# A first norm summed from channel blocks, a last norm's sum moved, and x loaded on another queue: two transformer blocks on one core

## The chip, the cores and the metric

The kernel runs on one NeuronCore of a Trainium2 chip. The metric is the device time of one execution in microseconds (us). The engines are named as the profile names them: PE (TensorE, matmul; PEld its weight loads), ACT (ScalarE), DVE (VectorE), POOL (GpSimd), SP (SyncE, which mostly issues DMAs).

## The reference

Two blocks run one after the other on one sequence of 256 tokens of 1024 channels, in float32. The first block has two layers; each is a gated feed-forward, a hybrid mixer, a second feed-forward and a small gated embedding. The second block has a mixer and a feed-forward with a norm before and a norm after it. What matters here is where norms stand:

```python
def rmsnorm(x, g):
    y = xf * lax.rsqrt(jnp.mean(xf * xf, axis=-1, keepdims=True) + EPS)
    return y.astype(x.dtype) * g

# first thing of the program
h = h + 0.5 * swiglu(rmsnorm(h, ffn1_norm[i]), ffn1_wg[i], ffn1_wu[i], ffn1_wd[i])

# last thing of the program
h = rmsnorm_2(x, norm_mlp_pre[l])
f = jnp.square(jax.nn.relu(h @ w_up[l])) @ w_down[l]
x = x + rmsnorm_2(f, norm_mlp_post[l])
```

`swiglu(x, wg, wu, wd)` is `(silu(x @ wg) * (x @ wu)) @ wd`; the feed-forward width is 2816 in the first block and 4096 in the second.

## The kernel before, in words

**Layout.** The stream h lies in SBUF as eight channel blocks (128 channels on the partitions, 256 tokens along the free axis). All weights are cut into 4948 tiles of 128x128 and laid out in DRAM in the order of use, so that one stream of DMAs reads them. The stream comes in pieces: one of 2 tiles, one of 4, then pieces of 8 tiles (512 KB). They are called w0, w1, w2, ... below (`PIECES`, `feed`). The first six land in buffers named `extra`, the later ones in four buffers named `raw`.

**Precision.** A product in float32 is made of three fast matmuls. ACT rounds a piece to its high part (`whi`), DVE subtracts to get the low part (`wlo`); the activations are split in the same way into `hs` (`split_scaled`: the high part on ACT, the low part on DVE). Then each tile takes three matmuls: high by high, high weight by low activation, low weight by high activation (`mm3`, line 237). Five pairs of `whi` and `wlo` exist, so that the piece five later can be split only when PE is through with the older one.

**Order.** The order of instructions on each engine is not written out by hand: generators run against a small clock model (`Flow`) which emits an instruction when the model says that its operand is there. Each engine then runs its list strictly in order. A DMA is issued by the engine whose `dma_start` is called.

**The first norm.** A norm's factor is one number per token, so the matmuls run on h times the gain, and the factor is applied behind them. Elsewhere in the kernel, `square` adds the squares of the eight blocks into a tile `acc` (squares on ACT, sums on DVE), and `colsum` sums over the partitions with matmuls against a tile of ones; their result lies in the bank `side`. For the first norm the kernel before does neither: it loads x a second time, with tokens on the partitions (`xt`, 1 MB, issued behind piece w6), and `first_sums` squares and sums it on ACT in two instructions. In both ways `rsqrt` (DVE, small instructions) and `bcast` (matmuls against `ident` into `side`, then ACT into `row`) follow.

**x and the first matmuls.** x comes in four DMAs, x0 (block 0), x1 (block 1), x2 (blocks 2 and 3) and x3 (blocks 4 to 7), each issued by SP behind the piece of the same number. The first four units (two gates, two ups, `heads_of`) are computed together: for each of the eight blocks, twelve matmuls. w0 and w1 thus hold 18 matmuls, every later piece 24.

**The last norms.** `norm2` in `second` is the norm ahead of w_up_2. Its factor enters only behind w_down_2 (`sq`, waited for by `down` through `r2ev`). It is spawned ahead of w_up_2, with its column sum among the matmuls of w_up_2.

Of the kernel before, what the change touches and what calls it, by code (L numbers as in the profile page):

```python
# [9 lines left out]
F32 = mybir.dt.float32  # L10
# [7 lines left out]
P = 128  # L18
T = 256
# [59 lines left out]
class Event:  # L79
    def __init__(self, on=False):  # L80
        self.on, self.waiting = on, []
# [110 lines left out]


class Build:
    def __init__(self, ctx, tc, xT, xtok, pT, vec, row, wall, out):
        self.tc, self.nc = tc, tc.nc
        self.xT, self.xtok, self.pT, self.vecd, self.rowd, self.wall, self.out = xT, xtok, pT, vec, row, wall, out
        self.flow = flow = Flow()
        self.spawn, self.fire, self.idle = flow.spawn, flow.fire, flow.idle
        pool = lambda name, bufs, **k: ctx.enter_context(tc.tile_pool(name=name, bufs=bufs, **k))  # L200
        self.fix = pool("fix", 1)
        self.big = pool("big", 1)
        self.dram = pool("dram", 2, space=DRAM)
        ps = pool("ps", 1, space=PSUM)
        fix = lambda name, shape, dt=F32: self.fix.tile(shape, dt, name=name)
        ring = lambda name, n, shape, dt=F32: Ring(flow, [fix(f"{name}{i}", shape, dt) for i in range(n)])
        self.banks = Ring(flow, [ps.tile([P, 512], F32, name=f"bank{i}") for i in range(7)])
        self.side = Ring(flow, [ps.tile([P, 512], F32, name="side")])
        self.raws = ring("raw", NR, [P, S * P])
        self.parts = Ring(flow, [(fix(f"whi{i}", [P, S * P], F32R), fix(f"wlo{i}", [P, S * P], F32R)) for i in range(NB)])  # L210

        self.small = [fix(f"small{i}", [P, 8]) for i in range(6)]
        hs0 = fix("hs0", [P, ND, 2 * T], F32R)
        self.hs = Ring(flow, [hs0, fix("hs1", [P, ND, 2 * T], F32R)])
        self.t = ring("t", 4, [P, T])
        self.vv = ring("vv", 3, [P, T])
        self.cv = ring("cv", 6, [P, 16 + T])
        self.sq = ring("sq", 2, [P, T])
        self.acc = ring("acc", 3, [P, T])
        self.rows = ring("row", 4, [P, T])  # L220
        self.small += [None if i == 17 or 18 <= i < 24 else fix(f"small{i}", [P, 8]) for i in range(6, 24)]
        self.vec = fix("vec", [P, NV])
        self.h = fix("h", [P, ND, T])
        self.ident = fix("ident", [P, P])
        self.ones = fix("ones", [P, P])
        self.mask = fix("mask", [P, P])
        self.tb = fix("tb", [P, 4, 32])
        self.gsum = fix("gsum", [P, 8])
        self.shim = fix("shim", [P, 32])
        self.order = []  # L230
        self.table = None
        self.tables = Ring(flow, [None])
        self.roots = Ring(flow, [None])
# [52 lines left out]
    def feed(self):  # L286

        self.ready = [Event() for _ in PIECES]
        self.done = [Event() for _ in PIECES]
        self.at = [None] * len(PIECES)  # L290
        for q, cnt in enumerate(PIECES):
            raw = yield from self.raws.get()
            n, w = int(FIRST[q]), cnt * P
            self.nc.sync.dma_start(raw[:, :w], self.wall[n * P * P:(n * P + w) * P].rearrange("(p w) -> p w", p=P))
            if q < 4:
                a, b = ((0, 1), (1, 2), (2, 4), (4, 8))[q]
                self.nc.sync.dma_start(self.h[:, a:b, :], self.xT[:, a:b, :])
                self.spawn(self.x_here(a, b), self.flow.use("dma", 0.365 * (b - a)) + 2.2)
            if q == 6:
                self.xt = self.big.tile([P, 2, D], F32, name="xt", tag="ya")  # L300
                self.nc.sync.dma_start(self.xt, self.xtok)
                self.spawn(self.first_sums(), self.flow.use("dma", 2.9) + 2.35)
            if q == 9:
                self.nc.sync.dma_start(self.vec[:, self.early:], self.vecd[:, self.early:])
            wait = self.flow.use("dma", w * P * 4 / 360e3) + 2.35
            self.spawn(self.piece(q, raw, w), wait)
# [172 lines left out]
    def norm(self, s, rows, ev):  # L479

        c, y = self.small[8][:, :2], self.small[9][:, :2]
        yield s["ev"]
        self.chains += 1
        if "cols" in s:
            c = s["cols"]
        else:
            yield from self.colsum(s, EPS, D, c)
        yield from self.rsqrt(y, c)
        yield from self.bcast(rows, y)
        self.fire(ev)  # L490
        self.chains -= 1
# [8 lines left out]
    def setup(self):  # L500
        nc = self.nc
        self.early = a = 32
        nc.sync.dma_start(self.vec[:, :a], self.vecd[:, :a])
        self.xev = [Event() for _ in range(ND)]
        self.flow.use("dma", 1.8)
        make_identity(nc, self.ident)
        nc.vector.memset(self.ones, 1.0)
        nc.vector.memset(self.shim, 0.0)

        nc.vector.memset(self.mask, 0.0)  # L510
        nc.gpsimd.affine_select(out=self.mask, in_=self.mask, pattern=[[1, P]], compare_op=ALU.is_ge,
                                fill=NEG, base=0, channel_multiplier=-1)
        self.chains = 0
        self.started = [Event() for _ in PIECES]
        extra = self.big.tile([P, 6, S * P], F32, name="extra", tag="X")
        self.extra = [extra[:, i, :] for i in range(6)]
        more = self.big.tile([P, 8, 8], F32, name="more", tag="more")
        self.small[18:] = [more[:, i, :] for i in range(6)]
        self.raws.free[:0] = self.extra
        for cv in self.cv.free:  # L520
            nc.vector.memset(cv[:, :16], 0.0)
        self.act(self.small[0], self.ones[:, :8], AF.Silu)

    def first(self, op, gain):
        for n in range(ND):
            yield self.xev[n]
            yield from self.split_scaled(op, n, self.h[:, n, :], gain(n))

    def x_here(self, a, b):
        for n in range(a, b):  # L530
            self.fire(self.xev[n])
        yield 0.0

    def first_sums(self):

        out, xt = self.x_ms["cols"], self.xt
        for tt in range(2):
            yield self.act(xt[:, tt, :], xt[:, tt, :], AF.Square, accum_out=out[:, tt:tt + 1])
        yield self.ts(out, out, 1.0 / D, EPS)
        self.fire(self.x_ms["ev"])  # L540

    def ffn(self, layer, which, sp, s, next_gain):

# [434 lines left out]
    def second(self, sp, ss):  # L978
# [283 lines left out]
            yield self.mul(sq, y, y)  # L1262
            self.fire(r2ev)

        self.spawn(norm2())

        def relu(j, b):
            t = yield from self.t.get()
            yield self.act(t, b[:, :T], AF.Relu)
# [10 lines left out]
        for j in range(NF2):  # L1280
            b = bs[j] if j < H else (yield from self.unit("w_up_2", 0, j, nsp, ND))
            self.spawn(relu(j, b))
        self.drop(nsp)

        C = D // 2
# [56 lines left out]
    def main(self):  # L1342
        gain = lambda name, i: (lambda n: self.v(name, i, n))
        sp = yield from self.new_op()
        s = self.x_ms = dict(cols=self.small[23][:, :2], ev=Event())
        self.spawn(self.first(sp, gain("ffn1_norm", 0)))
        for i in range(DEPTH):
            sp, s = yield from self.ffn(i, 1, sp, s, gain("mix_norm", i))
            sp, s = yield from self.mixer(i, sp, s, gain("ffn2_norm", i))
            pop = Operand(self.big.tile([P, 2, 2 * T], F32R, name="p_sp", tag="xd1"))  # L1350
            self.spawn(self.load_p(i, pop))
            sp, s = yield from self.ffn(i, 2, sp, s, gain("ple_norm", i))
            last = i + 1 == DEPTH
            sp, s = yield from self.ple(i, sp, s, pop, None if last else gain("ffn1_norm", i + 1))
            if not last:
                s, = s
        yield from self.second(sp, s)
# [18 lines left out]

def build(nc):
    dram = lambda name, shape, kind="ExternalInput": nc.dram_tensor(name, shape, F32, kind=kind).ap()
    args = (dram("in_x", (P, ND, T)), dram("in_xt", (P, 2, D)), dram("in_p", (DEPTH, P, 2, T)), dram("in_vec", (P, NV)),
            dram("in_row", (1, D)), dram("in_w", (NTILES * P * P,)), dram("out_0", (P, 2, D), "ExternalOutput"))  # L1380
    with tile.TileContext(nc) as tc, ExitStack() as ctx:
        b = Build(ctx, tc, *args)
        b.run()
    return b.order


def pack(inputs, order):
# [27 lines left out]
    for n, (name, layer, k, blk) in enumerate(order):  # L1415
# [11 lines left out]
        views[q][:, n - FIRST[q]] = t  # L1427
    return {
        "in_x": chan(f["x"][0]),
        "in_xt": np.ascontiguousarray(f["x"][0].reshape(2, P, D).transpose(1, 0, 2)),  # L1430
        "in_p": np.stack([chan(f["p"][i, 0]) for i in range(DEPTH)]),
        "in_vec": vec,
        "in_row": np.ascontiguousarray(f["norm_mlp_post_2"]),
# [13 lines left out]
```

## Time and profile before

| | us |
|---|---|
| median of 3 runs | 1822.45 (1811.29 to 1824.0) |
| the profiled execution | 1822.13 |
| its span, first to last instruction | 1820.3 |
| PE busy | 1789.6 |
| DVE busy | 1318.0 |
| ACT busy | 1050.9 |

The span is nearly full of matmuls, so the time changes only where PE stands still, where its clock is low, or where matmuls are added or taken away. The DMA moves 343.83 MB at a mean of 189 GB/s.

### The profile page before, as it was taken

To read this page: it belongs to the slowest core of one execution; us is meant where nothing else is said; L and a number is where in the kernel's file an instruction comes from. 1 tells how busy PE (TensorE), PEld (TensorE's weight loads), DVE (VectorE), ACT (ScalarE), POOL (GpSimd) and SP (SyncE) were. 2 spreads that over 40 slices of the span, in tenths; PEclk is the share of its full clock that TensorE was granted. 3 is DMA by queue.
4 is the path that set the end of the run, shared out by engine and by line. 5 is a ranking of instruction groups with operands and counts; after the bars stand their busy time and mean duration, and the time that the engine had idled before them with its cause. 6 is when DMAs were issued, how large, how long until landed. Compare 5 with 4: busy or idle time off the path is not lost.

```text
span 1820.3 us, 36518 instructions
## 1 busy us (share of the span) xinstructions
PE 1789.6 (98%) x14900; PEld 1749.2 (96%) x14900; DVE 1318.0 (72%) x2236; ACT 1050.9 (58%) x1707; POOL 10.5 (1%) x22
## 2 busy tenths in 40 slices
PE   8999999999999999999999999999999999989997
PEld 7999999999999999999999999999999999889986
DVE  6666789887676666866678988767666689877643
ACT  5444579664555544654457966455554478656542
POOL 0000000000000000000000000000000000000000
PEclk9999999999999999999999999999999999989999
DMA  7666576655666666566657656466666653546552
GB/s 254 192 186 188 169 244 197 199 196 160 201 194 191 192 196 195 176 198 196 195 172 248 196 198 196 161 194 198 203 194 195 195 176 123 183 140 207 187 195 76
DMA packets 92696, 343.83 MB, mean 189 GB/s; under 512 B 10448, under 2 KB 10960, under 8 KB 91376
## 3 DMA queue, kind: packets, MB, share of 16 engines
q1 hardware_dynamic: 90720, 327.25, 57.4%
q0 software_dynamic: 1520, 13.73, 2.1%
q8 instruction: 116, 1.90, 0.4%
q10 hardware_dynamic: 288, 0.52, 0.1%
q14 instruction: 52, 0.43, 0.1%
HBM read 340.31 MB, written 1.15 MB: 188 GB/s over the span
## 4 chain that ended last, share of the span: by engine, by line
PE 91%; DVE 4%; ACT 2%; DMA 2%; issue 1%; SPq 0%; DVEq 0%; ACTq 0%
PE bank L237 90%; DMA raw<-in_w 1%; DVE wlo L244 1%; PE side L237 1%; ACT L266 1%; ACT whi L266 0%; PE bank L734 0%; DMA h<-in_x 0%; DVE cv L257 0%; DVE small L257 0%; DVE hs L257 0%; DVE acc L244 0%; DVE t L244 0%; DVE vv L257 0%; DVE hs L244 0%
## 5 line engine op out<-in xcount | busy, mean ns | idle before, releaser
L237 PE MATMUL bank<-hs,whi 128*128 128x256 f32 x6928 | 1215.0, 280 | 12.4 <-ACT whi L266 7.9
L237 PEld LDWEIGHTS bank<-hs,whi 128*128 128x128 f32 x6928 | 1055.0, 189 | 19.6 <-ACT whi L266 8.2
L244 DVE TENSOR_TENSOR wlo<-raw,whi 128x1024 fp32r<-128x1024 f32 (+1 forms) x602 | 733.0, 1220 | 378.9 <-ACT whi L266 377.5
L266 ACT ACTIVATE whi<-raw 128x1024 fp32r<-128x1024 f32 (+1 forms) x602 | 635.3, 1058 | 637.4 <-issue 320.1
L237 PE MATMUL bank<-hs,wlo 128*128 128x256 f32 x3464 | 965.7, 279 | 1.9 <-DVE wlo L244 1.8
L237 PEld LDWEIGHTS bank<-hs,wlo 128*128 128x128 f32 x3464 | 655.5, 189 | 2.8 <-DVE wlo L244 2.7
L237 PE MATMUL bank<-V,whi 128*128 128x256 f32 x1920 | 329.0, 277 | 0.0
L237 PEld LDWEIGHTS bank<-V,whi 128*128 128x128 f32 x1920 | 290.4, 188 | 0.0
L237 PE MATMUL bank<-V,wlo 128*128 128x256 f32 x960 | 265.8, 277 | 0.0
L237 PEld LDWEIGHTS bank<-V,wlo 128*128 128x128 f32 x960 | 180.2, 188 | 0.0
L237 PE MATMUL bank<-whi,V 128*128 128x512 f32 x256 | 79.8, 392 | 0.0
L244 DVE TENSOR_TENSOR t<-bank,row 128x256 f32<-128x256 f32 x159 | 64.4, 417 | 17.2 <-PE bank L237 11.1
L257 DVE SCALAR_TENSOR_TENSOR cv<-bank,vec,cv 128x253 f32<-128x253 f32 (+2 forms) x144 | 63.6, 474 | 3.8 <-ACT cv L266 3.2
L244 DVE TENSOR_TENSOR vv<-bank,t 128x256 f32<-128x256 f32 x152 | 62.6, 418 | 3.2 <-ACT t L266 2.9
L244 DVE TENSOR_TENSOR V<-vv,V 128x256 fp32r<-128x256 f32 x152 | 62.5, 420 | 1.5 <-ACT V L266 1.2
L266 ACT ACTIVATE V<-vv 128x256 fp32r<-128x256 f32 x152 | 60.1, 403 | 2.6 <-DVE vv L257 1.6
L237 PEld LDWEIGHTS bank<-whi,V 128*128 128x128 f32 x256 | 48.1, 188 | 10.7
L237 PE MATMUL bank<-wlo,V 128*128 128x512 f32 x128 | 50.1, 392 | 0.0
L266 ACT ACTIVATE dec<-dec,tb 128x256 f32<-128x256 f32 (+1 forms) x128 | 49.5, 445 | 0.1
L244 DVE TENSOR_TENSOR acc<-acc,sq 128x256 f32<-128x256 f32 x101 | 42.4, 420 | 8.6 <-ACT sq L266 8.0
L266 ACT ACT_TABLE_LOAD x37 | 47.5, 1283 | 1.3 <-PEq L1442 0.7
L266 ACT ACTIVATE hs<-h,vec 128x256 fp32r<-128x256 f32 x80 | 38.4, 498 | 11.9 <-DMA h<-in_x 7.1
(152 smaller groups left out, 1113.4 us busy)
## 6 DMA issues: line engine op xcount, KB each, us to landing
raw<-in_w SPq DMA_DIRECT2D x613, 512.0 KB, 4.3
dec<-cum_d POOLq DMA_DIRECT2D x8, 1536.0 KB, 10.0
extra<-in_w SPq DMA_DIRECT2D x4, 512.0 KB, 8.6
xt<-in_xt SPq DMA_DIRECT2D x1, 1024.0 KB, 11.5
h<-in_x SPq DMA_DIRECT2D x1, 512.0 KB, 8.6
praw<-in_p POOLq DMA_DIRECT2D x2, 256.0 KB, 4.5
gain<-in_row POOLq DMA_DIRECT2D x1, 512.0 KB, 4.7
out<-o SPq DMA_DIRECT2D x2, 256.0 KB, 2.7
```

The source lines that it names most:

```text
L237: self.nc.tensor.matmul(ps, w, x, start=start, stop=stop, **k)
L244: self.nc.vector.tensor_tensor(out, a, b, op=op)
L257: self.nc.vector.scalar_tensor_tensor(out, a, s, b, op0=op0, op1=op1)
L266: self.nc.scalar.activation(out=out, in_=a, func=func, **k)
```

## The change

x and the first 32 columns of the vector table are loaded by DMAs that ScalarE issues, all at the start of the program. The second copy of x and `first_sums` go away; the first norm takes its squares block by block (`square`), with a column sum on PE (`colsum`) like every other norm. `norm2` is spawned behind w_up_2's loop instead of ahead of it.

```diff
             if q < 4:
-                a, b = ((0, 1), (1, 2), (2, 4), (4, 8))[q]
-                self.nc.sync.dma_start(self.h[:, a:b, :], self.xT[:, a:b, :])
+                a, b = self.xpieces[q]
                 self.spawn(self.x_here(a, b), self.flow.use("dma", 0.365 * (b - a)) + 2.2)
-            if q == 6:
-                self.xt = self.big.tile([P, 2, D], F32, name="xt", tag="ya")
-                self.nc.sync.dma_start(self.xt, self.xtok)
-                self.spawn(self.first_sums(), self.flow.use("dma", 2.9) + 2.35)
...
         yield s["ev"]
         self.chains += 1
-        if "cols" in s:
-            c = s["cols"]
-        else:
-            yield from self.colsum(s, EPS, D, c)
+        yield from self.colsum(s, EPS, D, c)
...
         self.early = a = 32
-        nc.sync.dma_start(self.vec[:, :a], self.vecd[:, :a])
+        self.xpieces = ((0, 1), (1, 2), (2, 4), (4, 8))
+        nc.scalar.dma_start(self.vec[:, :a], self.vecd[:, :a])
+        for b, c in self.xpieces:
+            nc.scalar.dma_start(self.h[:, b:c, :], self.xT[:, b:c, :])
...
-    def first(self, op, gain):
+    def first(self, op, s, gain):
         for n in range(ND):
             yield self.xev[n]
             yield from self.split_scaled(op, n, self.h[:, n, :], gain(n))
+            self.spawn(self.square(s, self.h[:, n, :]))
...
-    def first_sums(self):
-
-        out, xt = self.x_ms["cols"], self.xt
-        for tt in range(2):
-            yield self.act(xt[:, tt, :], xt[:, tt, :], AF.Square, accum_out=out[:, tt:tt + 1])
-        yield self.ts(out, out, 1.0 / D, EPS)
-        self.fire(self.x_ms["ev"])
...
-        self.spawn(norm2())
-
         def relu(j, b):
...
             self.spawn(relu(j, b))
+        self.spawn(norm2())
         self.drop(nsp)
...
-        s = self.x_ms = dict(cols=self.small[23][:, :2], ev=Event())
-        self.spawn(self.first(sp, gain("ffn1_norm", 0)))
+        s = yield from self.new_sum()
+        self.spawn(self.first(sp, s, gain("ffn1_norm", 0)))
```

The first place is ACT's list, from the second of the eight activation splits on (`hs` is the split of a block, `whi` of a piece; `acc` and `sq` are the new squares).

```order
 L266 ACTIVATE hs_94<-h,vec 128x256
+L266 ACTIVATE acc_111<-h 128x256
 L266 ACTIVATE whi_80<-extra 128x512
-L266 ACTIVATE hs_94<-h,vec 128x256 x2
+L266 ACTIVATE sq_109<-h 128x256
+L266 ACTIVATE hs_94<-h,vec 128x256
 L266 ACTIVATE whi_82<-extra 128x1024
-L266 ACTIVATE hs_94<-h,vec 128x256 x2
+L266 ACTIVATE hs_94<-h,vec 128x256
+L266 ACTIVATE sq_110<-h 128x256
+L266 ACTIVATE hs_94<-h,vec 128x256
+L266 ACTIVATE sq_109<-h 128x256
```

Piece w2 (`whi_82`) stood behind the splits of blocks 2 and 3; now it stands behind block 2's alone, and squares stand between the splits. Ahead of these rows ACT's list now begins with five DMA issues (the vector table, x0 to x3), in front of the load of its function table.

Behind them the list goes on with the later pieces; the split of the last block (`hs`) was ahead of the piece in `raw_74`, and is now behind two pieces from `raw`.

```order
 L266 ACTIVATE whi_78<-extra 128x1024
 L266 ACTIVATE hs_94<-h,vec 128x256
-L266 ACTIVATE xt,more<-xt 128x1024 x2
-L266 ACTIVATE whi_80<-raw_74 128x1024
-L266 ACTIVATE whi_82<-raw_75 128x1024
-L266 ACTIVATE whi_84<-raw_76 128x1024
+L266 ACTIVATE sq_109<-h 128x256
+L266 ACTIVATE whi_80<-raw_74 128x1024
+L266 ACTIVATE whi_82<-raw_75 128x1024
+L266 ACTIVATE hs_94<-h,vec 128x256
+L266 ACTIVATE sq_110<-h 128x256
+L266 ACTIVATE whi_84<-raw_76 128x1024
```

The two large squares of `xt` are gone, and block 7's split moved two pieces back (the `hs` in the first lines is block 6's in the new list, block 7's in the old).

The second place is PE's list in the first feed-forward of the changed kernel, at its 103rd matmul.

```order
L237 MATMUL bank_70<-hs_94,whi_78 128x256 x2
L237 MATMUL bank_70<-hs_94,wlo_79 128x256
L237 MATMUL side<-ones,acc_111 128x128 x2
L237 MATMUL bank_70<-hs_94,whi_78 128x256 x2
L237 MATMUL bank_70<-hs_94,wlo_79 128x256
```

Before, no column sum stood there. The matmuls against `ident` follow 29 matmuls later, as the 132nd; before they stood as the 136th.

The third place is PE's list at the start of w_down_2 in the changed kernel.

```order
L237 MATMUL bank_67<-whi_78,V_17740 128x512
L237 MATMUL bank_67<-wlo_79,V_17740 128x512
L237 MATMUL bank_67<-whi_78,V_17740 128x512
L237 MATMUL side<-ones,acc_113 128x128 x2
L237 MATMUL bank_68<-whi_80,V_17740 128x512
L237 MATMUL bank_68<-wlo_81,V_17740 128x512
```

`norm2`'s column sum now stands behind w_down_2's first six matmuls; before it stood among w_up_2's.

## Rows read from the trace of the kernel before

**Rows 1.** The page's first part: busy time, share, instructions of each engine.
```profile
PE 1789.6 (98%) x14900; PEld 1749.2 (96%) x14900; DVE 1318.0 (72%) x2236; ACT 1050.9 (58%) x1707; POOL 10.5 (1%) x22
```
**Rows 2.** Waits of PE, whole span: waiter, waited for, us, times, longest.
```profile
PE bank L237 <- ACT whi L266: 7.9, 2, 5.2
PE side L237 <- DVE small L257: 2.3, 1, 2.3
...
PE side L237 <- DVE acc L244: 1.3, 1, 1.3
```
**Rows 3.** ACT in order of time, first 20 us: start, duration, operation, idle before.
```profile
4.38 0.51 ACT L266 ACTIVATE hs<-h,vec 128x256 fp32r<-128x256 f32 x1 [2.14 <-DMA h<-in_x]
...
10.53 0.91 ACT L266 ACTIVATE hs<-h,vec 128x256 fp32r<-128x256 f32 x2 [4.06 <-DMA h<-in_x]
...
13.06 0.91 ACT L266 ACTIVATE hs<-h,vec 128x256 fp32r<-128x256 f32 x2 [0.68 <-DMA h<-in_x]
...
15.22 1.99 ACT L266 ACTIVATE whi<-extra 128x1024 fp32r<-128x1024 f32 x2
17.11 0.49 ACT L266 ACTIVATE hs<-h,vec 128x256 fp32r<-128x256 f32 x1
```
**Rows 4.** The chain that ended last, in three places: start, us, what.
```profile
3.54 6.97 DMA h<-in_x
...
11.44 0.95 ACT whi L266
...
12.41 1.24 DVE wlo L244
...
13.70 16.22 PE bank L237 x115
...
1619.06 0.73 PE side L237 x4
...
1622.04 1.24 PE side L237 x4
...
1640.68 0.44 PE side L237 x4
```
**Rows 5.** SP's DMA issues, first 5 us: start, us, operation.
```profile
0.74 0.38 SPq L503 DMA_DIRECT2D vec<-in_vec  x1
...
3.54 0.43 SPq L297 DMA_DIRECT2D h<-in_x  x1
4.01 0.43 SPq L294 DMA_DIRECT2D extra<-in_w  x1
```
**Rows 6.** DMA issues of w3 (window 4.0 to 4.4 us): KB each, us to landing.
```profile
extra<-in_w SPq DMA_DIRECT2D x1, 512.0 KB, 7.8
```
**Rows 7.** Windows: stretch, us, busy (instructions) of PE, PEld, DVE, ACT, POOL; clock, DMA, GB/s.
```profile
2.00:5.00 3.00, 0.00 (x0) 0.00 (x0) 0.08 (x1) 0.85 (x4) 0.00 (x0) 1.00 0.70 230
5.00:7.50 2.50, 2.26 (x9) 2.10 (x10) 1.92 (x4) 1.22 (x3) 0.00 (x0) 1.00 0.87 197
10.50:13.50 3.00, 0.51 (x2) 0.30 (x2) 1.97 (x3) 2.29 (x5) 0.00 (x0) 0.93 1.02 416
...
5.20:9.76 4.56, 4.51 (x18) 4.06 (x18) 1.72 (x4) 1.03 (x2) 0.00 (x0) 1.00 0.91 260
12.42:13.68 1.26, 0.51 (x2) 0.30 (x2) 1.26 (x2) 0.62 (x2) 0.00 (x0) 0.77 1.03 423
13.69:19.62 5.93, 5.92 (x27) 5.93 (x28) 5.08 (x7) 4.15 (x7) 0.00 (x0) 0.50 1.02 420
19.62:29.90 10.28, 10.28 (x91) 10.28 (x91) 5.21 (x15) 4.80 (x7) 0.00 (x0) 0.99 0.64 211
```
**Rows 8.** Windows, as in rows 7: early in w_down_2.
```profile
1725.00:1730.00 5.00, 5.00 (x24) 4.09 (x23) 1.96 (x3) 2.12 (x2) 0.00 (x0) 1.00 0.53 171
```
**Rows 9.** The page's costliest groups: DVE's addition of a square; its mean in ns.
```profile
L244 DVE TENSOR_TENSOR acc<-acc,sq 128x256 f32<-128x256 f32 x101 | 42.4, 420 | 8.6 <-ACT sq L266 8.0
```
**Rows 10.** ACT's square of a block, in order of time near 1626 us.
```profile
1625.85 0.40 ACT L266 ACTIVATE acc<-h 128x256 f32<-128x256 f32 x1
```

More of the change, by code (lines that the diff above doesn't have):

```diff
@@ L194, with __init__ @@
 class Build:
-    def __init__(self, ctx, tc, xT, xtok, pT, vec, row, wall, out):
+    def __init__(self, ctx, tc, xT, pT, vec, row, wall, out):
         self.tc, self.nc = tc, tc.nc
-        self.xT, self.xtok, self.pT, self.vecd, self.rowd, self.wall, self.out = xT, xtok, pT, vec, row, wall, out
+        self.xT, self.pT, self.vecd, self.rowd, self.wall, self.out = xT, pT, vec, row, wall, out
         self.flow = flow = Flow()
@@ L1378, in build @@
     dram = lambda name, shape, kind="ExternalInput": nc.dram_tensor(name, shape, F32, kind=kind).ap()
-    args = (dram("in_x", (P, ND, T)), dram("in_xt", (P, 2, D)), dram("in_p", (DEPTH, P, 2, T)), dram("in_vec", (P, NV)),
+    args = (dram("in_x", (P, ND, T)), dram("in_p", (DEPTH, P, 2, T)), dram("in_vec", (P, NV)),
             dram("in_row", (1, D)), dram("in_w", (NTILES * P * P,)), dram("out_0", (P, 2, D), "ExternalOutput"))
@@ L1429, in pack @@
         "in_x": chan(f["x"][0]),
-        "in_xt": np.ascontiguousarray(f["x"][0].reshape(2, P, D).transpose(1, 0, 2)),
         "in_p": np.stack([chan(f["p"][i, 0]) for i in range(DEPTH)]),
```

## The prediction

> **What bounds the kernel now.** I read the page's busy times first. PE is busy for 1789.6 of 1820.3 us [rows 1], so only the other 30.7 us, a low clock, or added matmuls can move the time. Next come PE's waits [rows 2]. Of 7.9 us that matmuls wait for weights' high parts, 5.2 is the start of the program (nothing can run earlier); the remaining 2.7 lies in the first 14 us. Then I read ACT in order of time there [rows 3], and the chain [rows 4]. They tell one story: x2 lands at 3.54 + 6.97 = 10.51, ACT wakes at 10.53 after 4.06 us of idleness, splits blocks 2 and 3 (0.91), then piece w2 (0.95). DVE makes w2's low part (1.24), and PE goes on at 13.70. PE had stopped at 9.76, when the 18 matmuls of w0 and w1 were done, and got only two matmuls in between [rows 7].
>
> The windows add the clock [rows 7]. From 13.69 to 19.62 the granted clock is 0.50 (1.2 GHz) and 28 matmuls take 5.93 us, 0.212 each; from 19.62 on it is 2.4 GHz and one takes 10.28 / 91 = 0.113. In 5.20 to 9.76 the record says 1.00, but 18 matmuls in 4.5 us is the lower pace. After 19.62 PE waits for nothing near the start.
>
> **The change, part by part.** Sums are made against the profiled 1822.13 us, 0.3 under the median of the three runs.
>
> *x's DMAs.* SP issued one DMA every 0.47 us, and x2 stood seventh, at 3.54 [rows 5]. On ScalarE it is fourth: 0.74 + 3 x 0.47 = 2.15, so 1.4 us earlier. But what x2 gains is set by the 16 DMA engines. Their busy share was 0.70 from 2 to 5 us and 0.87 from 5 to 7.5 [rows 7]; the room left is 3 x 0.30 + 2.5 x 0.13 = 1.2 us. With the same bytes ahead of it, x2 lands 1.2 us sooner, at 9.3. With w3 (4.01 + 7.8 = 11.8 [rows 5, 6]) also served before it, it lands 1.2 us before w3 did, at 10.6. The trace has no stretch at the start with two queues loading, so I take the middle, 9.95, and keep both ends.
>
> The Trainium skill ("DMA: Bandwidth & Descriptors", "Issuing engines are not separate DMA queues") speaks against this edit: issuing from more engines saves the sequencer's time alone. By that rule the transfers gain only what the engines had idle, which the busy shares above bear out; the rival "x comes no sooner" below is its strictest reading.
>
> *ACT's order.* In the new list only block 2's split stands between x2's landing and w2's split. From landing to PE's going on took 13.70 - 10.51 = 3.19 us [rows 4]; without one of two splits (0.91 / 2) it is 2.74. PE then goes on at 9.95 + 2.74 = 12.7, which is 1.0 us sooner; between 12.04 and 13.34 by the two ends, 1.65 to 0.35 us sooner. I let the clock behave as before: 5.93 us at the low level after the stop, so that all that follows moves by the same 1.0. **-1.0.**
>
> *Five DMA issues ahead of ACT's table load* push the first split from 4.38 back by 0.2 us: the issues take 5 x 0.47 = 2.35, the table load and a small operation 1.5 behind them, so 0.74 + 2.35 + 1.5 = 4.6 [rows 3, 5]. The first square (0.40 [rows 10]) stands ahead of w1's split. So w0's and w1's 18 matmuls end at 9.76 + 0.6 = 10.4. That lies inside the stop, which lasts to 11.4 (high parts) and 12.7: nothing. Without a stop it would cost 0.6.
>
> *Squares.* Eight on ACT at 0.40 and seven additions on DVE at 0.42 [rows 9, 10] replace two large ones of xt. They cost PE something only where PE overtakes. From x3's landing ACT now does, up to block 7's split, four block splits (0.91 a pair), three squares, and w3 to w7 (0.95 to 1.0 each [rows 3, 4]): 1.8 + 1.2 + 5.0 = 8.0, and 0.5 for DVE's part, 8.5 in all. Before it was 17.11 - 13.06 + 0.5. x3 landed at 13.06 [rows 3]; by the two ends it lands at 11.9 or, with one more 512 KB piece ahead (524 KB at 416 GB/s [rows 7], 1.3 us), at 13.2. With the later, block 7 is ready at 21.7. PE needs it for its 85th matmul. Before, 18 + 2 + 28 = 48 were done at 19.62 [rows 7], so 36 more at 0.113 put that at 23.7; now at 22.7. Slack 1.0: nothing.
>
> *The column sum* is four passes on PE, 0.44 us where the clock is up, as at 1640.68 [rows 4]. **+0.44.** Its input: behind block 7's split (21.2) ACT does one square, w8's high part and the last square, then DVE one addition: 0.4 + 1.0 + 0.4 + 0.42, ready at 23.4. PE is there after 102 matmuls, at 18.6 + 54 x 0.113 = 24.7. Slack 1.3. Behind PE's wait, were there one, all of PE's list would stand. The factor's chain from a column sum's end to the broadcast's start took 1622.04 - 1619.79 = 2.25 us [rows 4]; 29 matmuls lie between them here, 3.3 us. Slack 1.0. Nothing.
>
> *xt's DMA and ACT work* (1 MB, 2.5 us of transfers at 416 GB/s) go, but PE waits for nothing after 19.62: nothing.
>
> *norm2.* Its column sum (0.44 at 1640.68) leaves w_up_2 and joins w_down_2 at the same price. It saves no wait: PE's 1.3 us for an `acc` [rows 2] ends at 1619.06 and belongs to the norm behind w_o_2. The factor is wanted only after w_down_2's first half: 186 further matmuls at 5.0 / 24 = 0.208 [rows 8], 39 us, against a chain of 2.25 on a DVE busy for 1.96 of 5 us there. Zero on both sides.
>
> **Sum:** -1.0 + 0.44 = -0.56, so 1822.13 - 0.56 = 1821.6 us. By the ends alone, 1820.9 to 1822.2.
>
> **The rivals.**
>
> *The stop vanishes.* If w2's high part is made by 10.4, hence x2 and w2 have landed by 9.0, PE runs through. For it: everything through x3 is issued by 3.1 us. Against it: from 5 to 7.5 us the engines were 0.87 busy for 197 GB/s alone, less than half of the later 416 [rows 7]; it must be faster with two queues. Then PE starts at 5.5, and if its clock rises 5.9 us later as before, at 11.4, it has done 23 matmuls; 25 more at 0.113 bring the 48th to 14.2 instead of 19.62. -5.4 + 0.44: 1817.1 us. Chance 0.25.
>
> *The stop is shorter and the clock is not lost.* The record shows the fall to 0.50 only in the last part of the stop (0.77 over 12.42 to 13.68, then 0.50 [rows 7]). If a shorter stop leaves the clock up, the 28 slow matmuls cost 0.113 instead of 0.212 each, 2.8 less: 1818.8. Against it: the 18 before the stop ran at the lower pace. Chance 0.15.
>
> *x comes no sooner.* The two queues share the engines packet by packet, x1 lands with w2, x2 with w3, and the stop is only cut in two; PE goes on at 13.70 and the column sum is added: 1822.6. For it: the engines' high share. The Trainium skill (the same page, "Queues, rings and completion order") has each engine take whole packets from its queues in turn, which is this case; no run here shows it yet. Chance 0.15.
>
> *x3 comes late (the slower side).* Three pieces issued by SP can now overtake x3. Block 7's split then is what PE waits for. The point is x3's landing at 22.7 - 8.5 = 14.2 us; from 14.7 the kernel is slower. With two pieces more ahead of it than in my later end (13.2 + 2.6 = 15.8), PE waits 1.6: -1.0 + 1.6 + 0.44, 1823.2. Against it: x3 is issued by ScalarE's fifth issue, at 2.6. Chance 0.10.
>
> The forecast itself has 0.35.
>
> **How the numbers follow.** All cases lie between 1817.1 and 1823.2, within 0.3% of before. The program's own runs lie further apart (1811.29 to 1824.0), so the range takes these in at both sides: 1811 to 1825. About 1% (18 us) is what a measurement of this kernel can tell from no change; no case comes near it. Even the whole idle time of PE within the first 14 us and the low clock up to 19.62 are under 15 us. Faster by over 1%: 0.02; within 1%: 0.96; slower: 0.02, for what I have not seen.
>
> **What would show it.** In the profile after: ScalarE's issues one behind the other from 0.74, the first split near 4.6; ACT's wait for h near 10 us shorter than 4.06; PE's stop from about 10.4 to 11.4, low parts from 12.7; the clock back up near 18.6; a column sum near 25 us and no wait of PE on `acc` or `small` there; no PE wait on `hs` before its 85th matmul; in w_up_2 and w_down_2 no new wait. The forecast is wrong if PE does not stop at all (gain of some 5 us), if a second wait stands at block 7 or at the column sum, or if anything changes beyond the first 30 us and the moved sum.

## The result, and the profile after

The changed kernel takes 1810.2 us (median of 14 runs, 1806.1 to 1813.2); the kernel before took 1822.1 in the same session (14 runs, 1811.3 to 1824.6). The ratio is 0.994, with a 95% interval of 0.9927 to 0.9953: 11.9 us less, 0.65%. The profiled execution of after took 1810.08 us with a span of 1808.3, 12.0 us under the span of before. So the time stayed within 1%, as forecast, but the change brought 12 us where the sum said 0.56, and the median lies 0.8 us under the lower end of the range given (1811). Only about a quarter of the gain lies in the first 30 us, where the prediction looked. Of all the executions reported here two, both of the kernel that has x alone on ScalarE's queue, took 4.6 and 7.7 ms and are left out of its figures.

The page of after, busy times, to be held against [rows 1]:

```profile
PE 1778.2 (98%) x14904; PEld 1737.8 (96%) x14904; DVE 1320.9 (73%) x2243; ACT 1050.3 (58%) x1711; POOL 10.5 (1%) x22
```

PE executes four records more and is busy 11.4 us less. Its waits hardly changed: here are PE's waits of after (waiter, waited for, us, times, longest), to be held against [rows 2]. The 7.9 us for high parts became 7.3, and the wait for `acc` is still there.

```profile
PE bank L237 <- ACT whi L266: 7.3, 2, 6.1
...
PE bank L237 <- DVE wlo L244: 1.9, 4, 0.8
PE side L237 <- DVE acc L244: 1.2, 1, 1.2
```

So the same matmuls became faster. Where, the long pieces of the chain tell (start, us, what, how many records), first of before, then of after:

```profile
30.36 178.79 PE bank L237 x1518
...
212.77 42.76 PE bank L237 x363
...
1641.12 132.69 PE bank L237 x900
```
```profile
22.75 0.44 PE side L237 x4
...
26.82 172.74 PE bank L237 x1524
...
203.28 41.15 PE bank L237 x363
...
1616.69 90.93 PE bank L237 x773
1707.62 0.44 PE side L237 x4
```

178.79 / 1518 is 117.8 ns for a matmul of 256 columns; 172.74 / 1524 is 113.3. In the next piece it is 42.76 / 363 = 117.8 against 41.15 / 363 = 113.4. These are unbroken pieces of PE, without a wait, and the granted clock is 1.00 in both kernels. (The pieces of 900 and 773 can't be divided like this: the first takes in matmuls of 512 columns, the second begins with 24 matmuls at the low clock and ends with six of 512 columns. For these the windows tell the pace.) Windows show the same in w_gate, w_up and in w_up_2 (stretch, us, busy and instructions of PE, PEld, DVE, ACT, POOL; clock, DMA share, GB/s), before and then after:

```profile
100.00:120.00 20.00, 20.00 (x172) 20.00 (x171) 12.14 (x18) 9.57 (x14) 0.00 (x0) 1.00 0.63 186
...
1650.00:1670.00 20.00, 20.00 (x172) 20.00 (x171) 15.47 (x26) 12.53 (x22) 0.00 (x0) 1.00 0.68 213
```
```profile
100.00:120.00 20.00, 20.00 (x179) 20.00 (x178) 12.89 (x19) 9.57 (x14) 0.00 (x0) 1.00 0.71 199
...
1650.00:1670.00 20.00, 20.00 (x179) 20.00 (x178) 13.95 (x24) 12.82 (x22) 0.00 (x0) 1.00 0.64 206
```

172 matmuls in 20 us against 179, at one and the same granted clock. (A window also counts the two or three matmuls that reach over its edges, so the chain gives the truer quotient.) I call the two paces slow (117.8 ns) and fast (113.4 ns). The Trainium skill ("TensorE: Matmul & The Clock Gate", "Back-to-back issue gap") gives 262 cycles for 256 columns as the gap of an isolated matmul, which at 2.4 GHz I estimate at 109.2 ns; it adds that in a stream of weight loads and matmuls the spacing is set by both together. The trace has 272 and 283 cycles of 2.4 GHz, so neither pace is that figure.

**The ledger.** How far after is ahead, at the same instruction of both:

| place | gain there, us | ahead, us |
|---|---|---|
| behind the first broadcast and 135 tile matmuls (30.36; 26.82 + 6 x 0.113 = 27.50) | 2.9 | 2.9 |
| the 1518 matmuls that follow, up to the next column sum: 1518 x 4.45 ns | 6.7 | 9.6 |
| 24 matmuls between two groups (after is at the slow pace here) | -0.1 | 9.5 |
| 363 matmuls up to 255.53 (244.43 in after) | 1.6 | 11.1 |
| from there to the column sum behind w_o_2 (1619.06; 1610.42) | -2.5 | 8.6 |
| the broadcast behind it (1.24; 0.72) | 0.5 | 9.2 |
| w_up_2: 660 matmuls x 4.5 ns, and the moved sum's 0.44 | 3.4 | 12.6 |
| the moved sum in w_down_2, up to the end | -0.6 | 12.0 |

Of the 2.5 us that are given back between 255 and 1619 us, 1.2 is the stretch of 321 matmuls ahead of that column sum, 41.1 us in after (slow) and 39.9 in before (fast); the pace changes back and forth in both kernels. The other 1.3 lies in small pieces that I didn't follow.

What changes the pace? In the timelines of before and after it changes, from the clock's rise up to 255 us, only where `side` stands in PE's list, at a group of two float32 128x128 matmuls (four records): a column sum or a broadcast. In before the first norm has one such group (the broadcast at 29.91), and the pace goes from fast to slow there. In after it has two: at the column sum (22.75) it goes from fast to slow, at the broadcast (26.38) from slow to fast. The last norm's column sum, alone in w_up_2 of before, left the rest of w_up_2 slow. From this came my theory: **the pace of PE's stream is reset by each float32 group**, and the change shifts the pattern of groups. Its rivals: the gain comes with x's loads, or with the work that is gone on ACT and DVE.

### The profile page after: what moved, and what is told of

Its sections match the earlier page's. It is cut to its first block, busy times and chain, and to the rows that moved or that the text cites. A ratio compares the mean times of both kernels' runs of the same rounds, so it can differ in the third digit from the quotient of the medians.

```text
span 1808.3 us, 36543 instructions
## 1 busy us (share of the span) xinstructions
PE 1778.2 (98%) x14904; PEld 1737.8 (96%) x14904; DVE 1320.9 (73%) x2243; ACT 1050.3 (58%) x1711; POOL 10.5 (1%) x22
## 4 chain that ended last, share of the span: by engine, by line
PE 91%; DVE 4%; DMA 2%; ACT 2%; issue 1%; ACTq 0%; DVEq 0%; SPq 0%
PE bank L237 90%; DVE wlo L244 1%; DMA raw<-in_w 1%; PE side L237 1%; DVE cv L257 1%; ACT whi L266 0%; ACT L266 0%; PE bank L722 0%; DMA h<-in_x 0%; DVE small L257 0%; DVE hs L257 0%; DVE dec L244 0%; DVE acc L244 0%; DVE t L244 0%; DVE vv L244 0%
## 5 line engine op out<-in xcount | busy, mean ns | idle before, releaser
L237 PE MATMUL bank<-x,raw 128*128 128x256 f32 x208 | 45.2, 379 | 0.0
```

What stands on the lines that cost most here:

```text
L237: self.nc.tensor.matmul(ps, w, x, start=start, stop=stop, **k)
```

## The parts of the change, one at a time

**Only x on ScalarE's queue** (`xt`, `first_sums` and `norm2` as before):

```diff
-                self.nc.sync.dma_start(self.h[:, a:b, :], self.xT[:, a:b, :])
...
-        nc.sync.dma_start(self.vec[:, :a], self.vecd[:, :a])
+        nc.scalar.dma_start(self.vec[:, :a], self.vecd[:, :a])
+        for b, c in ((0, 1), (1, 2), (2, 4), (4, 8)):
+            nc.scalar.dma_start(self.h[:, b:c, :], self.xT[:, b:c, :])
```

> The kernel before with x and the first vector columns issued by ScalarE at the start; the second copy of x and its two large squares stay, norm2 stays. This is the part that my prediction priced at -1.0 us. From the traces PE is some 3.0 us ahead at its 135th matmul of tiles in the changed kernel, the column sum included: so 3 us less here, 1819 us, with the stretch from 27 to 206 us at 117.8 ns as before (toggle: one broadcast alone, slow). Load, if the place of x's DMAs is what counts: 113.3 ns there and 1811 us.

Measured: 1818.1 us (median of eight runs, 1809.1 to 1820.0) against 1820.8, ratio 0.9978 (0.9953 to 1.0002); the interval takes in no change. Five of the eight lie between 1817.5 and 1820.0 and three between 1809.1 and 1810.6; the profiled one is of the five. Its chain at the first broadcast and behind it:

```profile
25.84 0.44 PE side L237 x4
26.28 178.79 PE bank L237 x1518
```

The broadcast begins 4.1 us sooner than in before (29.91), and 2.7 us or more sooner than in the four other profiles whose start is that of before (28.5 to 30.2). So the load makes the gain of the start. The 1518 matmuls behind it take 178.79 us, to the last digit what they took in before: the load does not make the fast pace.

**Only the squares and the column sum** (x issued by SP as before, `xt` gone, `norm2` at its old place):

```diff
+            self.spawn(self.square(s, self.h[:, n, :]))
...
-        if "cols" in s:
-            c = s["cols"]
-        else:
-            yield from self.colsum(s, EPS, D, c)
+        yield from self.colsum(s, EPS, D, c)
```

> The squares of x's channel blocks and their column sum alone: x still comes by SP's queue, xt is gone, the last norm's sum stands in w_up_2 as before. PACE BY GROUPS: the column sum near 28 us and the broadcast behind it are two groups of float32 matmuls; the matmuls after the broadcast run at 113.4 ns up to the next column sum near 202 us, w_up_2 still at 117.9. The stretch of 1881 matmuls gives 8.3 us back, the column sum costs 0.44: about 1814 us, 8 under before, with x2's stop (PE going on near 12.5 to 13.7) unchanged. LOAD (x's queue makes the gain): 1822.5, 0.4 above before, the stretch at 117.8.

Measured: 1816.7 us median, runs from 1812.9 to 1823.9, ratio 0.9988 (0.9967 to 1.001). The medians are 5.3 us apart where 8 was expected, and the interval takes in no change. The profile (1816.76 us) shows the expected pace:

```profile
28.98 172.74 PE bank L237 x1524
```

So the fast pace comes without x's new load. Four of the ten runs lie at 1820.8 or above. A pace drawn anew in each execution would explain that, but an execution without a profile doesn't show its pace.

**Only `norm2` moved** behind w_up_2's loop:

```diff
-        self.spawn(norm2())
-
         def relu(j, b):
...
+        self.spawn(norm2())
         self.drop(nsp)
```

> The kernel before with norm2 spawned behind w_up_2's loop, nothing else. Toggle: the first stretch is as slow as before (117.8 ns from 30 to 209 us, which also says that the pace repeats from execution to execution), and in w_up_2 the 660 matmuls behind 1640 us that took 117.9 ns take 113.4: 3.0 us less, 1819 us. My prediction (the sum only changes its place): 1822 us and 117.9 ns or no difference between the two. Drawn anew: the first stretch may come out at either pace.

Measured: 1819.3 us median against 1820.8, ratio 0.9995 (0.9978 to 1.0012): by the times nothing that can be told. The chain shows that the first norm's stretch is slow as before, and a window of w_up_2 that this is fast, as in after:

```profile
28.94 178.79 PE bank L237 x1518
```
```profile
1650.00:1670.00 20.00, 20.00 (x179) 20.00 (x178) 14.79 (x24) 12.94 (x22) 0.00 (x0) 1.00 0.68 212
```

## Groups that nobody reads

If groups alone set the pace, a group whose result nobody reads must do it too.

**One group added to before**, behind the first broadcast:

```diff
         yield from self.bcast(rows, y)
         self.fire(ev)
         self.chains -= 1
+        if not self.grouped:
+            self.grouped = True
+            for _ in range(1):
+                yield from self.idle_group()
...
+    def idle_group(self):
+        b = yield from self.side.get()
+        for tt in range(2):
+            w = self.mm(b[:, tt * P:(tt + 1) * P], self.ident, self.ones, cost=0.213)
+        yield w
+        self.side.put(b)
```

> The kernel before with one extra group of two float32 matmuls (128 columns each, ident by ones into side, read by nobody) some ten matmuls behind the first norm's broadcast; nothing else is changed. In the trace of before, 1518 matmuls behind that broadcast start 117.8 ns apart, in the changed kernel 113.3 ns. Theory 'toggle' (each group on side leaves PE at the other of two paces, so one group alone leaves it at the slow one): the pace is 113.4 ns from the extra group to about 247 us, 1518 x 4.5 + 363 x 4.6 = 8.5 us less, 0.4 more for the group: 1814 us. Rival 'load' (the slow pace comes from what the old start does: the second copy of x, the order of ACT and DVE): still 117.8 ns, 1822.5 us. Rival 'drawn anew' (the pace is drawn in each execution): either, and the times of the rounds spread over both.

Measured: 1815.9 us against 1820.8, ratio 0.998 (0.9963 to 0.9998): with added work the kernel is a little faster. The chain ahead of the broadcast, and behind it:

```profile
18.95 10.72 PE bank L237 x91
...
30.36 1.72 PE bank L237 x15
32.08 0.44 PE side L237 x4
32.52 170.36 PE bank L237 x1503
```

170.36 / 1503 = 113.3 ns. But the way there was not the one expected: ahead of the broadcast the pace was slow (10.72 / 91 = 117.8), where before's profile had 0.113 [rows 7], the broadcast already made it fast, and the added group left it so. So this profile does not show that the added group changes a pace; it does show that the pace behind the clock's rise is not fixed, for up to the broadcast PE's list is that of before.

**The same group added to after:**

> The changed kernel with the same extra group behind the first norm's broadcast. Toggle: PE is at the slow pace, 117.8 ns, from about 27 us to the next column sum near 205, and then the other way round up to the transposes at 250: about 1518 x 4.5 + 1.7 + 0.4 = 8.9 us more, 1819 us. Load: 113.3 ns stays, 1810.6 us. Drawn anew: either.

Measured: 1809.5 us, ratio 0.9948 (0.993 to 0.9965): it gains over before what after gains. A theory by which a third group turns the pace to slow, whatever came before, has failed. The chain:

```profile
12.89 8.83 PE bank L237 x75
...
26.05 1.06 PE bank L237 x9
...
27.55 171.72 PE bank L237 x1515
```

Here too the start was slow (8.83 / 75 = 117.7); the column sum made it fast, the broadcast slow (1.06 / 9 = 0.118), the added group fast again (171.72 / 1515 = 113.3). A group mostly changes the pace it finds, and the pace at the start differs between executions of kernels that are the same up to there. Whether it differs between two executions of one program, no profile shows: after alone was profiled twice, and was fast there both times.

**Half a group** (one float32 matmul instead of two), in before and in after, at the same place:

```diff
+        for tt in range(1):
+            w = self.mm(b[:, tt * P:(tt + 1) * P], self.ident, self.ones, cost=0.213)
```

> Before, with half a group (one float32 128x128 matmul, two records, 0.22 us) that nobody reads behind the first broadcast. ONE MATMUL IS ENOUGH: the pace goes from 117.8 to 113.4 ns behind it, for 1881 matmuls up to the column transposes near 250 us: 8.3 - 0.2, about 1814 to 1816 us. TWO ARE NEEDED (or the second matmul undoes what the first does): the stretch stays at 117.8, 1822.3 us, 0.2 above before.

> The changed kernel, with half a group (one float32 128x128 matmul that nobody reads) behind the first broadcast. Start, loads and the order of the real work stay as in the changed kernel. PACE BY GROUPS: the half group takes the pace from 113.4 to 117.8 ns, as it did in the kernel before with half a group; 1524 matmuls up to the next column sum lose 6.7 us and, where that sum or the broadcast behind it does not set it back at once, 363 more lose 1.6: 1817 to 1818.5 us. LOAD OR ORDER (the gain comes from how x is loaded, or from the work that is gone): 1810.4 us, 0.2 above the changed kernel.

Measured in before: 1820.4 us, 0.9992 (0.998 to 1.0005). Measured in after: 1817.1 us (1813.4 to 1822.2), against 1809.8 (1807.8 to 1812.6) for the changed kernel on the same chip. Chain of before with half a group, then of after with it:

```profile
30.68 1.72 PE bank L237 x15
...
32.62 177.02 PE bank L237 x1503
```
```profile
23.19 3.18 PE bank L237 x27
...
26.81 1.04 PE bank L237 x9
...
28.07 178.44 PE bank L237 x1515
```

The first missed its expectation that half a group makes a slow stretch fast: the broadcast had already made it fast (1.72 / 15 = 115 ns), and the half group made it slow (177.02 / 1503 = 117.8). That told what to expect of the second, and it came: 178.44 / 1515 = 117.8 behind the half group. After keeps its loads, squares and order and loses 7.2 us by one matmul of 0.2 us. This leaves nothing of the rival that x's loads or the lighter ACT make the long gain: here both are there and the stretch is slow, and in before with one group added both are missing and the stretch is fast.

**One group added in w_up_2** of before, right behind `norm2`'s column sum, which stays where it is:

```diff
             yield from self.colsum(ns, EPS, D, c)
+            yield from self.idle_group()
```

> Before, with one more group of two float32 128x128 matmuls that nobody reads, right behind the last norm's column sum in w_up_2; the sum stays where it is. PACE BY GROUPS: behind the sum the pace is 117.9 ns for a few matmuls, behind the added group 113.4, so w_up_2 ends 2.9 us sooner and the group costs 0.44: 1819.6 us, 2.5 under before. PLACE (it is the sum's place in w_up_2, or the norm's work on the other engines, that slows w_up_2): w_up_2 stays at 117.9, 1822.5 us, 0.4 above before.

Measured: 1818.1 us against 1822.0, ratio 0.9979 (0.9963 to 0.9994). The chain within 1643 to 1700 us, of this kernel and then of before:

```profile
1642.90 57.12 PE bank L237 x504
```
```profile
1642.89 57.12 PE bank L237 x485
```

504 matmuls against 485 in the same 57.12 us: 113.3 and 117.8 ns. Here, too, the way was another than expected: the timeline has the slow pace ahead of the column sum, the sum itself made the stream fast, and the added group left it so. The gain of some 3 us comes with the pace, at the old place of the sum; so it is not the place that slows w_up_2. What the added group does there this run doesn't show, since it met the fast pace. Of the five groups or half groups that nobody reads, three changed the pace (one in after, both halves) and two left the fast pace that they met (both in before).

## The start: can more be had?

**x0 and x1 by SP as before, x2 and x3 by ScalarE**, since x1 came late in after (below):

```diff
                 a, b = self.xpieces[q]
+                if q < 2:
+                    self.nc.sync.dma_start(self.h[:, a:b, :], self.xT[:, a:b, :])
...
-        nc.scalar.dma_start(self.vec[:, :a], self.vecd[:, :a])
-        for b, c in self.xpieces:
+        nc.sync.dma_start(self.vec[:, :a], self.vecd[:, :a])
+        for b, c in self.xpieces[2:]:
```

> The changed kernel, with vec, x0 and x1 issued by SP between w0, w1 and w2 as before, x2 and x3 by ScalarE as in the change. STOP AT x1: PE starts at 5.3 instead of 6.13, and the stop of 1.2 us at 7.9 goes, since x1 lands near 5.4 instead of 7.7; x2 lands near 9 and its stop is short. All behind the first 12 us comes 1 to 2 us sooner, the paces as in the changed kernel: 1808.5 us, 1.5 under the changed kernel and 13.5 under before. NOTHING (the stop is only moved to x2, or two queues deliver the same bytes no sooner): 1810.2, as the changed kernel; PE would then stop near 9.8 up to 11.

Measured: 1811.1 us (1807.8 to 1817.9, 6 runs), ratio 0.9945 (0.9923 to 0.9967): no better than after. The stop at x1 did go, but not as expected. x0 itself now lands late, at 1.65 + 5.15 = 6.8, behind x2 and x3 of the other queue (4.8 and 6.5), and PE begins at 7.76 instead of 6.13:

```profile
1.65 5.15 DMA h<-in_x
...
7.76 9.80 PE bank L237 x65
...
26.31 172.74 PE bank L237 x1524
```

The stretch behind the broadcast begins at 26.31 against 26.82: half a microsecond, less than the executions differ.

**Idle matmuls on PE while it waits for the first piece**, in after:

```diff
+        for _ in range(11):
+            nc.tensor.matmul(self.side.free[0][:, :P], self.ones, self.ones, start=True, stop=True)
```

> The changed kernel, with eleven float32 128x128 matmuls of a constant (ones by ones, nobody reads them) on PE at the program's start, while it waits for the first piece up to 6.13 us. CLOCK AT THE START: PE is busy from about 1.3 us instead of 6.13, so the granted clock rises sooner than 14.05 us; of the 42 matmuls that run at 0.213 us up to there, 20 to 40 run at 0.113, less what PE then waits for x1 and the next weights: 2 to 4 us under the changed kernel, 1806 to 1808 us, with the paces of 113 ns behind the broadcast as in the changed kernel. NOTHING (PE then waits for pieces as much longer as it runs faster): 1810.2 us. If the first norm's two groups leave the pace at 117.8 here, 8 us more than either.

**The changed kernel once more**, on the same chip:

> The changed kernel itself once more, beside the other two, for a direct comparison and a second look at its paces. PACE BY GROUPS, with the pace behind the clock's rise drawn anew: 113.4 ns behind the first broadcast if the start is at 113.4 (as in the first profile), 1810 us; 1817 to 1818 us in an execution whose broadcast falls back to 117.8. LOAD OR ORDER: 1810 us in every execution, whatever the pace behind the broadcast.

Measured: 1812.3 us (1809.3 to 1816.9) with the idle matmuls and 1809.8 (1807.8 to 1812.6) without, 6 runs each: no gain. The second profile of after shows the same piece as the first, 172.74 us for 1524 records from 27.16 on. Windows of the kernel with idle matmuls:

```profile
4.00:6.00 2.00, 1.89 (x11) 1.70 (x10) 0.45 (x2) 1.42 (x4) 0.00 (x0) 1.00 0.97 339
6.00:8.00 2.00, 1.17 (x6) 0.79 (x6) 0.37 (x2) 0.52 (x2) 0.00 (x0) 1.00 0.99 384
8.00:10.00 2.00, 1.13 (x4) 0.91 (x5) 1.64 (x4) 2.00 (x5) 0.00 (x0) 0.67 1.03 420
10.00:12.00 2.00, 2.00 (x11) 2.00 (x11) 1.77 (x3) 2.00 (x6) 0.00 (x0) 0.50 1.03 420
12.00:14.00 2.00, 2.00 (x19) 2.00 (x19) 2.00 (x5) 2.00 (x4) 0.00 (x0) 0.98 1.03 416
```

The idle matmuls do bring the clock up sooner, and then PE waits 1.7 us for x1's block (in 6 to 10 us it is busy for 2.30 of 4), the granted clock falls to 0.50 (1.2 GHz) and comes back near 12. (The expectation's 42 matmuls ahead of 14.05 us are a misreading: 27 start there in after.) The stretch behind the broadcast begins at 25.99, 0.8 us sooner than in after. In this execution w_up_2 was slow, and that cost four times as much. The chain within w_up_2, of this kernel and then of after:

```profile
1619.97 80.09 PE bank L237 x680
```
```profile
1639.95 60.07 PE bank L237 x530
```

80.09 / 680 = 117.8 ns; 60.07 / 530 = 113.3. No version among these beats the changed kernel.

## Why the prediction was right in its bound and wrong in its reasons

**Right:** that the time stays within 1%, that no wait of PE stands at block 7, at the column sum or at the broadcast, that `xt`'s work was hidden, that the squares cost nothing, and that a column sum's own duration is 0.44 us (22.75 and 1707.62 in after). Its own falsifier came true: something changed "beyond the first 30 us and the moved sum". That the forecast of 1% held says little for the sum: the gain is some twenty times the 0.56 us that it gives. And 1% was too coarse for what a measurement can tell: with 14 runs of each kernel the interval of the ratio, 0.9927 to 0.9953, excludes no change.

**Wrong, the step that cost the most: "so that all that follows moves by the same 1.0".** The sum priced a column sum by its duration alone, and took the matmuls behind it at the duration they had before. The missing term is the pace: 6.7 - 0.1 + 1.6 = 8.2 us up to 255 us, although one group more costs 0.44. The trace of before showed both paces, and I read past it: 10.28 / 91 = 0.113 in [rows 7], but 1518 records in 178.79 us right behind, 0.118. I had used the first for all that follows 19.62.

**Wrong: "Zero on both sides" for norm2.** The sum's duration moved at its own price, as said. But it had left 660 matmuls of w_up_2 at the slow pace: 3.0 us. (Two counts of the prediction are misread, without weight for the sum: in [rows 7] 27 matmuls, not 28, stand in the low stretch, 28 is PEld's count; and the 24 of [rows 8] take in matmuls that reach over the edges, their starts lie 0.229 us apart and not 0.208.)

**Mis-sized: the start.** -1.0 + 0.44 was forecast; the row says -2.9, the 0.44 included. The steps, by rows of after. ACT in order of time (start, duration, operation, idle before) and the first long piece of the chain:

```profile
1.18 1.90 ACTq L498 DMA_DIRECT2D h<-in_x  x4
3.11 1.28 ACT L266 ACT_TABLE_LOAD   x1 [3.11 <-issue]
...
5.27 0.51 ACT L266 ACTIVATE hs<-h,vec 128x256 fp32r<-128x256 f32 x1 [0.66 <-DMA h<-in_x]
...
7.72 0.51 ACT L266 ACTIVATE hs<-h,vec 128x256 fp32r<-128x256 f32 x1 [1.64 <-DMA h<-in_x]
...
9.27 0.49 ACT L266 ACTIVATE hs<-h,vec 128x256 fp32r<-128x256 f32 x1
```
```profile
1.66 6.04 DMA h<-in_x
...
9.11 13.64 PE bank L237 x96
```

- *x's DMAs.* x2 was to land at 9.95, between 9.3 and 10.6. It landed at 8.4 (issued at 2.14, 6.3 us to landing), sooner than both ends: ACT makes block 2's split at 9.27 without waiting. Three issues of after, w2, x2 and x1 (KB each, us to landing):

```profile
extra<-in_w SPq DMA_DIRECT2D x1, 512.0 KB, 5.9
h<-in_x ACTq DMA_DIRECT2D x1, 256.0 KB, 6.3
h<-in_x ACTq DMA_DIRECT2D x1, 128.0 KB, 6.0
```

The bound that failed is "the room left is 1.2 us". I took 1 minus the engines' busy share for all the room there was. The windows of after say otherwise, to be held against the same stretches in [rows 7]:

```profile
2.00:5.00 3.00, 0.00 (x0) 0.00 (x0) 0.00 (x0) 1.49 (x2) 0.00 (x0) 1.00 0.83 243
5.00:7.50 2.50, 1.37 (x6) 1.32 (x6) 0.82 (x2) 0.81 (x2) 0.00 (x0) 1.00 0.96 349
```

From 5 to 7.5 us the busy share rose from 0.87 to 0.96, and the rate from 197 to 349 GB/s (250 in the other profile with x on SP's queue, that of squares and column sum alone). So a busy share of 0.87 did not mean that little more would fit. Most of x2's 2.1 us is its sooner issue: 1.4 us (2.14 instead of 3.54), with 6.3 us to landing against 7.0 in before and 6.5 in that other profile. The Trainium skill's rule ("DMA: Bandwidth & Descriptors", "Issuing engines are not separate DMA queues") leaves a second issuing engine just this, the sequencer's time; so the rule fits within 0.7 us, and what failed is my reading that the engines' idle share caps it. The same page ("Queues, rings and completion order") has each DMA engine serve its queues in turn. No row here shows the turns themselves, but in the next point x1 and x0 take longer with two queues loading.

- *The stop.* It is not where the sum has it. The rival "x comes no sooner" named it: x1 lands with w2. x1 landed at 1.66 + 6.04 = 7.70, w2 at 1.65 + 5.9 = 7.55; in before x1 took 2.8 us. PE stops from 7.9 to 9.11 for x1's block and w1's high part, and not again; so that rival was right on x1, and wrong on x2 and on the time. The rival "the stop vanishes" had its condition on the landings met (x2 and w2 by 9.0; w2's high part was made at 10.7, not by 10.4), and still PE stopped, at x1.
- *Five DMA issues on ACT.* The table load ends later, as said (4.61 with the small operation), but the first split stands at 5.27: it waits for x0, which takes 4.0 us instead of 2.6. PE begins 0.9 us later. "Inside the stop: nothing" is wrong, since the stop at x2 is gone.
- *The clock.* I took 5.93 us at the low level behind the stop. In after the low level ends at about 14.0 instead of 19.62, as windows of after show: 21 matmuls in 4.90 us up to there (the row says 1.00, but 0.233 each is the lower pace), 77 in 8.50 behind it. 27 matmuls have been made by then where before made 48, so 21 run at 0.113 instead of 0.21: 2.1 us. With 2.2 us for the shorter stop (3.4 us without a matmul in before, 1.2 now) and 0.9 lost by PE's later start that is 3.4 us; less the column sum's 0.44 it is the row's 2.9.

```profile
9.10:14.00 4.90, 4.89 (x21) 4.67 (x22) 4.67 (x9) 4.90 (x11) 0.00 (x0) 1.00 1.03 417
14.00:22.50 8.50, 8.50 (x77) 8.50 (x76) 8.50 (x13) 7.31 (x11) 0.00 (x0) 1.00 0.69 248
```

**The range** reached down to 1811 because the program's own runs did. That spread was a hint not followed: of 28 runs of before beside the first experiments, 4 lie between 1812.5 and 1815.0 and 24 between 1818.7 and 1825.6. (In the 29 runs of before beside the next experiments there is no such gap: they lie at 1809.4, 1813.1, 1815.4, 1815.4, 1816.3, 1817.1 and from 1818.7 on.) The two paces over 1518 + 363 matmuls differ by 8.4 us. An execution of before whose start is slow would have its one group make the stream fast; the profile of before with half a group shows just that at its broadcast. That this is what happened in the four runs is argued, since none of them has a profile. Against it stands that none of after's 20 runs lies above 1813.2, though by the same argument a slow start, which the profile of after with a group added has, should cost after some 7 us.

## What to carry to other kernels

Divide the long, unbroken pieces of PE in the chain by their counts, one by one: where two pieces of the same matmul differ by 4% at the same granted clock, the difference over hundreds of matmuls outweighs most edits, and an added or moved float32 matmul can turn it either way. Price such an edit by what follows it, not by its own duration, and where runs of one program seem to fall into two clusters, look for a stretch whose length times the difference is the distance between them. A small gain found this way can turn with the next edit upstream: take away or add one such matmul to see whether the gain belongs to the edit at all.

## What the runs showed of the hardware that was not expected

PE's stream of weight loads and 128x256 matmuls has two stable paces at a granted clock of 1.00: 113.3 to 113.4 ns and 117.8 to 117.9 ns from start to start, each kept for up to 1524 matmuls without a change. In the thirteen profiles of this case the pace changed, in the first 256 us, at nearly every float32 group: of 26 groups that met the slow pace 23 left the fast one, and of 24 that met the fast pace 23 left the slow one. The exceptions are the column sum that follows next behind a half group (in both kernels that have one), a column sum 2.1 us behind a break of the stream (in the kernel with idle matmuls), and the group added behind the first broadcast of before. Later in the program a group that meets the fast pace can leave it so. The pace right behind the clock's rise was fast in some profiles (before: 0.113 in [rows 7]) and slow in others (10.72 / 91 = 0.118 with a group added behind it, where PE's list ahead of it is the same). Half a group changes it as well. The four float32 32x32 transposes near 250 us left the fast pace in all thirteen profiles, whether they met the slow one (four) or the fast one (nine), so not every float32 matmul turns it back and forth. In the kernel with idle matmuls the pace changed at that short break, near 19.7 us. What in PE's queue differs between the two paces no run here shows: the durations of the weight loads are the same in both (188 ns), only their distance differs. Whether a group that is not float32 would change the pace wasn't tried.
